# A block of the in-projection of a hybrid decoder layer: plain columns turned into seven-product form, column sets interleaved, and the token sums built from unsplit rows

## The chip, the cores and the metric

The kernel runs on one core of one Trainium2 chip. The metric is device time in microseconds (us) of one execution, the median of several; lower is better. The engines are named as in the profile: PE (matrix products), PEld (loading of PE's stationary operand), DVE (elementwise vector work), ACT (scalar functions and copies), POOL (here it issues DMAs that add into what lies at their destination), SP (issues ordinary DMAs).

## The reference, cut to what matters

One layer of a decoder on 512 tokens of width 2048. The in-projection feeds two mixers; the change touches the part of it that makes `v`.

```
shift, scale, gate = silu(c) @ W_ada + b_ada          # c: one row of 2048
h = RMSNorm(x) * (1 + scale) + shift                  # 512 x 2048
[q_lat | kv_lat | k_rope | z_mla | u | v | z_sgu | g_mla | g_sgu] = h @ W_in
    # widths 768, 512, 64, 2048, 2048, 2048, 2048, 2048, 2048
A = causal latent attention(q_lat, kv_lat, k_rope) * silu(z_mla)
B = u * (tril(W_s) @ rmsnorm(v) + b_s) * silu(z_sgu)  # chunks of 128 tokens
x = x + gate * ((sigmoid(g_mla) * A + sigmoid(g_sgu) * B) @ W_out)
out = RMSNorm(x)
```

## The kernel before, in words

**Precision.** A product of float32 matrices is made of three PE products: each operand is a high part (`hi`, rounded) and a low part (`lo` = operand minus `hi`), and `mm3` (L150 to L153) adds hi*hi, hi*lo and lo*hi into one bank of PSUM (the accumulators of PE). In the blocks below the same three stand at L638.

**The stream of weights.** Class `Stream` (L70 to L130) holds a list of granules, each up to 128 x 1024 values of a weight. A granule's raw values come by DMA into one of a few raw tiles; then it is *split*: ACT copies it into the high part (the cast, L121) and DVE subtracts that from the raw values (the low part, L122). `get(i)` splits granule i+1 while PE works on granule i, and lets DMAs run `look` granules ahead. There are two pairs of part tiles, `w0` and `w1`, so that a granule's split can't begin before PE is done with the one two places back. With `fine` the split is made in two halves; `after` keeps a granule's DMA back until another is split; `fetch` and `make` run extra DMAs or extra DVE work.

**Stages.** (1) The first weight group, `g1`. (2) The second, `g2`: 16 granules of 640 columns, one for each 128 of the 2048 rows of K. (3) The `v` stage, with which the change deals. (4) The pair stage: the other products of the in-projection, head by head, as a long row of slots of equal length. (5) Attention, the out projection, the last norm.

**Rows and fixes.** `h` is held as 16 tiles `hh[j]`, `hl[j]` (128 of K x 512 tokens). The shift of a tile is a dot product of silu(c) with a row block of W_ada on DVE (`ada_dot`, called by `dot_to`: 128 x 2048, L142). It is not there when the first products run, so `fix_to` (L464 to L491) builds the rows two tiles at a time: DVE makes `t` = x times gain and norm (two at L482 through the helper at L142), ACT adds the shift into the high parts (two at L489), DVE makes the low parts (two at L491, shown as L142). `FIXED` and `DOTS` are tables that say up to where fixes and dots have got at each granule: fixes stand in g2 at granules 4, 9, 12 and 14 and in the `v` stage at steps 0, 2, 4 and 5.

**The v stage.** 2048 columns of `v` and 64 of k_rope, 2112 in all. 1024 columns are one block made with seven products in the place of eight (2 x 2 x 2: token halves, K halves, column halves): products p1 to p7 take sums of weight quarters and sums of row quarters, each with 4 granules of two K tiles, 512 columns wide, 256 tokens. The other columns are plain: 8 granules of 384 columns, 8 more of 384, and 8 of 320, each with two K tiles and four token groups. Sums of weights are made by POOL's accumulating DMAs (p6, p2, p4) or on DVE (p3, 128 x 1024). Sums of rows (`make_sums`) are built on DVE from `hh` + `hl`: two adds of 512 and four of 256 for each of eight tiles, and then split. The stage's order is the list `plan`: 16 plain steps of 384, p1, half of the 320 ones, p6, the other half, p2, two steps for the first gate's product of head 14 (`z`), p7 and p3 in turns, p5, p4. The last four steps stand in a loop of their own at the head of the pair stage (L1357). Beside the stage, `lat_scale` (DVE, 128 x 512, 13 times) scales the latent rows and stores them, and each finished quarter of `v` is combined on DVE, squared and summed on ACT, and stored.

Of the kernel before, what the change touches and what calls it, by code (L numbers as in the profile page):

```python
# [38 lines left out]
VW = (384, 384, 320)  # L39
# [21 lines left out]
class Stream:  # L61
# [40 lines left out]
    def split_to(self, i):  # L102
        i = min(i, len(self.src) - 1)
        while self.n_split <= i:
# [6 lines left out]
            if make is not None:  # L111
                make(raw)
# [19 lines left out]
def trunk_layer(ctx, tc, xT, xn, c, vecs, pos, wada, w1, w2, wv, wv3, wv4, wh, wh15, wq, wqr, wk, wvv, wo, wsT, bsp, gfin, out,  # L132
# [111 lines left out]
    g2 = [ws.add(w2[k], 640) for k in range(KC)]  # L244
    chain = [None] * 4

    def chain_load(i):
        chain[i] = nt(c1[0].p, [P, GW], F32, f"raw{4 + i}")
        DMA.dma_start(chain[i], wv[0, i])
        return chain[i]  # L250

    def adding(src, i):
        nc.gpsimd.dma_start(chain[i], src, accum_op=ALU.add)
        return chain[i]

    b22 = [None] * 4

    def hold(i, t):
        b22[i] = t
        return t  # L260

    def kept_raw(raw):
        ws.held += 1

    def add_kept(i, raw):
        tt(raw, raw, b22[i], ALU.add)
        ws.held -= 1

    gv, last_of, steps = [], {}, []
    plan = [(kind, i) for kind, n0, n1 in ((0, 0, 8), (1, 0, 8), ("p1", 0, 4), (2, 0, 4), ("p6", 0, 4), (2, 4, 8), ("p2", 0, 4))  # L270
            for i in range(n0, n1)]
    plan += [("z", 0), ("z", 1)] + [(kind, i) for i in range(4) for kind in ("p7", "p3")]
    plan += [(kind, i) for kind in ("p5", "p4") for i in range(4)]
    for kind, i in plan:
        if kind == "z":
            g = ws.add(wh[H - 2, 0, i], GW)
        elif kind in (0, 1, 2):
            g = ws.add((wv3[0], wv3[1], wv4)[kind][i], 2 * VW[kind])
        elif kind == "p1":
            g = ws.add(None, GW, fetch=lambda t, i=i: chain_load(i), fine=True)  # L280
        elif kind in ("p6", "p2", "p4"):
            src = {"p6": wv[1, i], "p2": wv[1, 4 + i], "p4": wv[0, 4 + i]}[kind]
            g = ws.add(None, GW, fetch=lambda t, i=i, src=src: adding(src, i), after=last_of[i], fine=True)
        elif kind == "p7":
            g = ws.add(wv[1, 4 + i], GW, fetch=lambda t, i=i: hold(i, t), make=kept_raw, fine=True)
        elif kind == "p3":
            g = ws.add(wv[1, i], GW, make=lambda raw, i=i: add_kept(i, raw), fine=True)
        else:
            g = ws.add(wv[0, 4 + i], GW, fine=True)
        if kind in ("p1", "p6", "p2"):  # L290
            last_of[i] = g
        gv.append(g)
        steps.append((kind, i))
    gq, gr, gk, gvv = {}, {}, {}, {}
    c1 = [None]
# [40 lines left out]
    xp = Scope("xT")  # L336
    psp = Scope("psA", space=PSUM)
# [62 lines left out]
    def square_of(j):  # L400
        if j == 0:
            ACT.activation(ssx, xt[j], AF.Square)
            return None
        sq = nt(xp.p, [P, S], F32, "sq", bufs=2)
        ACT.activation(sq, xt[j], AF.Square)
        return sq
# [63 lines left out]
    def fix_to(n, between=None):  # L470
# [12 lines left out]
        for j in js:  # L483
            t = nt(xp.p, [P, S], F32, "t", bufs=2)
# [37 lines left out]
    S3_AT, S4_AT = ("cosT", "lat8", "lat9", "lat0"), ("sinT", "lat1", "lat7", "lat2")  # L522
    halves_, s3f, s4f = {}, {}, {}

    def half_of(tags, j):

        if j % 2 == 0:
            halves_[tags, j // 2] = nt(latp.p, [P, S], F32, tags[j // 2])
        return halves_[tags, j // 2][:, (left, right)[j % 2]]

    def make_sums(j):
        a, b = (nt(tb.p, [P, S], F32, f"t{i}") for i in range(2))
        tt(a, hh[j].bitcast(F32), hl[j].bitcast(F32), ALU.add)
        tt(b, hh[j + 8].bitcast(F32), hl[j + 8].bitcast(F32), ALU.add)
        s3f[j], s4f[j] = half_of(S3_AT, j), half_of(S4_AT, j)
        tt(s3f[j], a[:, left], a[:, right], ALU.subtract)
        tt(b[:, right], a[:, right], b[:, right], ALU.subtract)
        tt(a[:, left], b[:, right], a[:, left], ALU.subtract)
        tt(s4f[j], a[:, left], b[:, left], ALU.add)

        def split():
            for name, src in (("s1", b[:, right]), ("s2", a[:, left])):
                hilo(sums[name + "h"][:, j], sums[name + "l"][:, j], src)

        return split

    def split_s4(j):
        hilo(sums["s4"][:, j, 0], sums["s4"][:, j, 1], s4f[j])

    def split_s3(j):  # L550
        hilo(hh[j][:, right], hl[j][:, right], s3f[j])
# [15 lines left out]
    for t_, i in zip((8, 9, 10, 11, 12, 13, 16, 17, 24, 25, 26, 28, 30), (8, 1, 9, 7, 12, 10, 0, 2, 3, 4, 11, 5, 6)):  # L567
        early.setdefault(t_, []).append(lambda i=i: lat_scale(i))

    def sums_begin(j, t_):  # L570
        early.setdefault(t_ + 1, []).insert(0, make_sums(j))

    for j, t_ in enumerate((9, 11, 12, 14, 15, 20, 21, 22)):
        early.setdefault(t_, []).append(lambda j=j, t_=t_: sums_begin(j, t_))
# [1285 lines left out]
```

## Time and profile before

| what | value |
|---|---|
| time, median of 3 runs (lowest, highest) | 1549.36 us (1549.21, 1549.51) |
| the profiled execution's own time | 1549.69 us |
| its span on the core | 1548.0 us |
| what lies around the span | 1.69 us |
| granted clock of PE, mean | 0.998 |
| g1 | 0 to 98.5 us |
| g2 | 98.97 to 153.81 us |
| v stage | 153.81 to 336.72 us |
| pair stage | 336.72 to about 1080 us |
| attention and out projection | about 1080 us to the end |

A row of the timeline gives start, duration, engine, line, operation, output<-inputs, shapes, and how many instructions it stands for; what stands in brackets is idle time ahead of it on its engine and what ended it. A row of groups gives count, then after the bar busy time in us, the mean of one in ns, and the idle time ahead. A row of windows gives the stretch, its length, and for PE, PEld, DVE, ACT and POOL the busy time (and instructions), then the granted clock, the busy share of the 16 DMA engines and GB/s.

### The profile page before, as it was taken

To read this page: it belongs to the slowest core of one execution; us is meant where nothing else is said; L and a number is where in the kernel's file an instruction comes from. 1 tells how busy PE (TensorE), PEld (TensorE's weight loads), DVE (VectorE), ACT (ScalarE), POOL (GpSimd) and SP (SyncE) were. 2 spreads that over 40 slices of the span, in tenths; PEclk is the share of its full clock that TensorE was granted. 3 is DMA by queue.
4 is the path that set the end of the run, shared out by engine and by line. 5 is a ranking of instruction groups with operands and counts; after the bars stand their busy time and mean duration, and the time that the engine had idled before them with its cause. 6 is when DMAs were issued, how large, how long until landed. Compare 5 with 4: busy or idle time off the path is not lost.

```text
span 1548.0 us, 27203 instructions
## 1 busy us (share of the span) xinstructions
PE 1535.9 (99%) x10680; PEld 1431.5 (92%) x10680; DVE 1176.7 (76%) x1808; ACT 764.4 (49%) x1331; POOL 104.6 (7%) x128
## 2 busy tenths in 40 slices
PE   9999999999999999999999999999999999999997
PEld 7888999889999999999999999999888888888887
DVE  8989787568787888877778777777788888854543
ACT  4443454555645454454555546555655555632322
POOL 0000001001111111111111111121000000000000
PEclk9999999999999999999999999999999999999999
DMA  9978387758999999997888888888544344245423
GB/s 376 386 272 311 121 241 220 178 177 210 279 267 280 251 250 252 267 264 206 222 234 251 221 246 242 223 204 219 164 143 131 129 125 145 81 163 189 136 82 109
DMA packets 129394, 327.57 MB, mean 212 GB/s; under 512 B 14809, under 2 KB 36337, under 8 KB 124529
## 3 DMA queue, kind: packets, MB, share of 16 engines
q1 hardware_dynamic: 112114, 270.52, 50.9%
q0 software_dynamic: 17008, 55.06, 19.8%
q8 instruction: 84, 1.38, 0.4%
q14 instruction: 44, 0.36, 0.1%
q10 hardware_dynamic: 144, 0.26, 0.1%
HBM read 301.85 MB, written 23.94 MB: 210 GB/s over the span
## 4 chain that ended last, share of the span: by engine, by line
PE 95%; DMA 2%; DVE 1%; ACT 0%; SPq 0%; issue 0%; DVEq 0%; ACTq 0%
PE ps L1410 15%; PE ps L1411 15%; PE ps L1412 15%; PE ps L152 14%; PE ps L153 14%; PE ps L151 14%; PE ps L638 4%; PE ps L1589 1%; PE ps L970 1%; DMA wraw<-in_w 1%; PE ps L1553 1%; PE ps L1552 1%; DMA half<-in_pos 1%; DMA v_d<-lat 0%; DMA wada<-in_wada 0%
## 5 line engine op out<-in xcount | busy, mean ns | idle before, releaser
L1410 PE MATMUL ps<-h,w2h 128*128 128x256 f32 x408 | 113.8, 279 | 0.0
L1410 PE MATMUL ps<-h,w0h 128*128 128x256 f32 x408 | 113.1, 277 | 0.7 <-DVE lat L139 0.7
L1412 PE MATMUL ps<-h,w2l 128*128 128x256 f32 x408 | 112.7, 276 | 0.0
L1412 PE MATMUL ps<-h,w0l 128*128 128x256 f32 x408 | 112.7, 276 | 0.0
L1411 PE MATMUL ps<-h,w2h 128*128 128x256 f32 x408 | 112.7, 276 | 0.0
L1411 PE MATMUL ps<-h,w0h 128*128 128x256 f32 x408 | 112.7, 276 | 0.0
L1410 PE MATMUL ps<-h,w1h 128*128 128x256 f32 x400 | 110.9, 277 | 0.0
L1412 PE MATMUL ps<-h,w1l 128*128 128x256 f32 x400 | 110.5, 276 | 0.0
L1411 PE MATMUL ps<-h,w1h 128*128 128x256 f32 x400 | 110.5, 276 | 0.0
L122 DVE TENSOR_TENSOR w0l<-wraw,w0h 128x1024 fp32r<-128x1024 f32 (+3 forms) x70 | 71.5, 1024 | 47.3 <-ACT w0h L121 47.0
L122 DVE TENSOR_TENSOR w1l<-wraw,w1h 128x1024 fp32r<-128x1024 f32 (+3 forms) x71 | 65.5, 928 | 51.0 <-ACT w1h L121 49.8
L121 ACT CAST w1h<-wraw 128x1024 fp32r<-128x1024 f32 (+3 forms) x71 | 57.4, 814 | 93.1 <-PE ps L153 33.1
L121 ACT CAST w0h<-wraw 128x1024 fp32r<-128x1024 f32 (+3 forms) x70 | 62.7, 899 | 81.7 <-PE ps L153 36.5
L139 DVE TENSOR_TENSOR w0l<-raw,w0h 128x1024 fp32r<-128x1024 f32 x56 | 68.5, 1224 | 32.6 <-ACT w0h L796 31.8
L151 PE MATMUL ps<-h,w1h 128*128 128x512 f32 x218 | 86.6, 397 | 0.0
L153 PE MATMUL ps<-h,w1l 128*128 128x512 f32 x218 | 85.0, 390 | 0.0
L152 PE MATMUL ps<-h,w1h 128*128 128x512 f32 x218 | 85.0, 390 | 0.0
L139 DVE TENSOR_TENSOR w1l<-wraw,w1h 128x1024 fp32r<-128x1024 f32 x44 | 53.9, 1225 | 36.4 <-ACT w1h L796 36.4
L139 DVE TENSOR_TENSOR w2l<-wraw,w2h 128x1024 fp32r<-128x1024 f32 x46 | 56.3, 1224 | 29.9 <-ACT w2h L796 29.8
L151 PE MATMUL ps<-h,w0h 128*128 128x512 f32 x198 | 78.0, 394 | 0.0
L152 PE MATMUL ps<-h,w0h 128*128 128x512 f32 x198 | 77.2, 390 | 0.5 <-DVE h L142 0.5
L774 POOL DMA_DIRECT2D wraw<-in_wh x55 | 49.3, 958 | 417.6 <-DVE w1l L139 153.3
(418 smaller groups left out, 5462.3 us busy)
## 6 DMA issues: line engine op xcount, KB each, us to landing
raw<-in_wh SPq DMA_DIRECT2D x104, 512.0 KB, 6.9
wada<-in_wada SPq DMA_DIRECT2D x31, 1024.0 KB, 6.8
wraw<-in_wh POOLq DMA_DIRECT2D x55, 512.0 KB, 8.3
wraw<-in_wh SPq DMA_DIRECT2D x45, 512.0 KB, 6.1
raw<-in_wh POOLq DMA_DIRECT2D x36, 512.0 KB, 7.5
wraw<-in_wo SPq DMA_DIRECT2D x32, 512.0 KB, 3.7
half<-in_w SPq DMA_DIRECT2D x35, 256.0 KB, 5.6
wraw<-in_w SPq DMA_DIRECT2D x16, 512.0 KB, 8.4
```

The costliest lines, as they stand in the source:

```text
L121: self.nc.scalar.copy(hi[:, sl], raw[:, sl])
L122: self.nc.vector.tensor_tensor(out=lo[:, sl], in0=raw[:, sl], in1=hi[:, sl].bitcast(F32), op=ALU.subtract)
L139: DVE.tensor_tensor(out=out, in0=in0, in1=in1, op=op)
L151: PE.matmul(ps, ah, bh, start=start, stop=False)
L152: PE.matmul(ps, ah, bl, start=False, stop=False)
L153: PE.matmul(ps, al, bh, start=False, stop=stop)
L638: PE.matmul(ps, x_[:, tk], w_[:, sl], start=st and m == 0, stop=c == 7 and m == 2, skip_group_check=True)
L774: q_.dma_start(t, wh[h, n, q // 10 - 1], **eng)
L970: PE.matmul(ps[:, n], v[:, n], wr[:, q], start=True, stop=True)
L1410: PE.matmul(ps[:, :256], wH[:, cols[c]], xh, start=c == 0 and first, stop=False, skip_group_check=True)
L1411: PE.matmul(ps[:, :256], wH[:, cols[c]], xl, start=False, stop=False, skip_group_check=True)
L1412: PE.matmul(ps[:, :256], wL[:, cols[c]], xh, start=False, stop=c == 7, skip_group_check=True)
```

## The change

All columns of `v` but 256 (320 with k_rope) are now made with seven products: set `a` (columns 0 to 1023, halves of 512) and set `b` (columns 1024 to 1791, halves of 384; these were the 16 plain granules of 384). Both sets use the same sums of rows. The plain 320 columns go first, the `z` product of head 14 next, and then the two sets in turns.

- **Order of the steps** (4 granules each but for v and z): v 0 to 7, z 8 and 9, a1 10 to 13, b1 14 to 17, a5 18 to 21, b5 22 to 25, a6 26 to 29, a7 30 to 33, a2 34 to 37, a3 38 to 41, a4 42 to 45, b6 46 to 49, b7 50 to 53, b2 54 to 57, b3 58 to 61, b4 62 to 65 (the last four in the loop at the pair stage's head).
- **Sums of weights.** a6: an ordinary load into a chain tile and an accumulating DMA onto it. a2, a4, b2, b4: an accumulating DMA onto the chain tile. a3, b3: an ordinary load and an accumulating one. b6: two ordinary loads, added on DVE (128 x 768). So 28 accumulating DMAs stand in the stage (16 of 512 KB, 12 of 384 KB) where 12 stood.
- **Sums of rows.** `fix_to` gets one more instruction for each tile: ACT writes t + shift back into `xt[j]`, so that the unsplit row stays. `make_sums` is then four DVE instructions of 256 for each of eight tiles, each using what the one ahead of it made, and `split_sums` four casts on ACT and four lows on DVE, one step later.
- **Side work.** `lat_scale` is moved to steps 8, 30 to 37, 42, 44, 46 and 48; the combining of quarters (`corner`) is put on numbered steps. `FIXED` and `DOTS` are unchanged.

```diff
-VW = (384, 384, 320)
+VW = {"a": 512, "b": 384, "v": 320}
+V0 = {"a": 0, "b": 1024, "v": 1792}
...
+    def onto(t, src):
+        nc.gpsimd.dma_start(t, src, accum_op=ALU.add)
+    def chain_load(i, c, n):
+        chain[i] = t = nt(c1[0].p, [P, GW], F32, f"raw{4 + i}")
+        DMA.dma_start(t[:, :n], wpair[c][0, i])
+        if c == "a":
+            onto(t[:, :n], wpair[c][1, i])
+        return t
+    def add_raw(i, raw, n):
+        tt(chain[i][:, :n], chain[i][:, :n], raw[:, :n], ALU.add)
         return chain[i]
...
+    steps = [("v", "", i) for i in range(8)]
+    for kind in ("z", "a1", "b1", "a5", "b5", "a6", "a7", "a2", "a3", "a4", "b6", "b7", "b2", "b3", "b4"):
+        steps += [(kind[0], kind[1:], i) for i in range(2 if kind == "z" else 4)]
...
         for j, t in zip(js, ts_):
             stt(hl[j], t, shift[:, j:j + 1], hh[j].bitcast(F32), ALU.add, ALU.subtract)
+            ACT.activation(xt[j], t, AF.Identity, bias=shift[:, j:j + 1])
...
     def make_sums(j):
-        a, b = (nt(tb.p, [P, S], F32, f"t{i}") for i in range(2))
-        tt(a, hh[j].bitcast(F32), hl[j].bitcast(F32), ALU.add)
-        tt(b, hh[j + 8].bitcast(F32), hl[j + 8].bitcast(F32), ALU.add)
-        s3f[j], s4f[j] = half_of(S3_AT, j), half_of(S4_AT, j)
...
+        u, v = xt[j], xt[j + 8]
+        a, b = temps[j] = [nt(xq.p, [P, S], F32, "t", bufs=2) for _ in range(2)]
+        tt(a[:, left], u[:, right], v[:, right], ALU.subtract)
+        tt(a[:, right], a[:, left], u[:, left], ALU.subtract)
+        tt(b[:, left], a[:, right], v[:, left], ALU.add)
+        tt(b[:, right], u[:, left], u[:, right], ALU.subtract)
+    def split_sums(j):
+        a, b = temps.pop(j)
+        s1, s2 = sums_of[j] = [nt(xp.p, [P, 2, 256], F32R, f"x{c}") for c in (j, j + 8)]
+        hilo(s1[:, 0], s1[:, 1], a[:, left])
+        hilo(s2[:, 0], s2[:, 1], a[:, right])
+        hilo(sums["s4"][:, j, 0], sums["s4"][:, j, 1], b[:, left])
+        hilo(hh[j][:, right], hl[j][:, right], b[:, right])
...
+    for j, t_ in enumerate((8, 9, 11, 13, 15, 18, 20, 23)):
+        at_step(t_, make_sums, j)
+        at_step(t_ + 1, split_sums, j)
+    for t_, i in zip((8, 30, 31, 32, 33, 34, 35, 36, 37, 42, 44, 46, 48), (11, 0, 2, 8, 9, 7, 1, 12, 3, 10, 4, 5, 6)):
+        at_step(t_, lat_scale, i)
+    for n in range(2):
+        for t_, f, *a in ((20, keep_v, "a", "1", n), (22, corner, "a", n, "11"), (24, keep_v, "b", "1", n), (26, corner, "b", n, "11"),
...
+                          (42, keep_v, "a", "3", n), (43, corner, "a", n, "22"), (46, corner, "a", n, "21"),
```

**Place 1: ACT at the second fix of g2.** `w0h` and `w1h` are high parts of weights, `wraw` a raw tile, `h` the high parts of the rows, `t` what DVE made for them. Before, ACT has:

```order
L121 CAST w0h_1225<-wraw_26_1159 128x640
L489 ACTIVATE h_137_1251<-t_1247,shift_88 128x512
L489 ACTIVATE h_138_1253<-t_1249,shift_88 128x512
L121 CAST w1h_1257<-wraw_27_1183 128x640
L121 CAST w0h_1281<-wraw_28_1207 128x640
```

After, on the same engine at the same place (`x` is the row tile that is kept, and the lines of the file have moved):

```order
L122 CAST w0h_1230<-wraw_26_1164 128x640
L495 ACTIVATE h_137_1256<-t_1252,shift_88 128x512
L495 ACTIVATE h_138_1258<-t_1254,shift_88 128x512
L500 ACTIVATE x_40_173<-t_1252,shift_88 128x512
L500 ACTIVATE x_41_174<-t_1254,shift_88 128x512
L122 CAST w1h_1264<-wraw_27_1188 128x640
L122 CAST w0h_1288<-wraw_28_1212 128x640
```

Two instructions have come in between the high parts of the rows and the next weight's cast.

**Place 2: DVE around b6 (steps 46 to 49).** `raw` is a chain tile, `wraw` the second load, `lat<-lat,rx` is `lat_scale`, `lat<-ps,lat` a corner; `x2` are the two halves of a split. Before, at the p7 and p3 steps, which held the DVE additions of weights there:

```order
L122 TENSOR_TENSOR w0l_2700<-w2l_2440,w0h_2699 128x512 x2
L139 TENSOR_TENSOR wraw_71_2475<-wraw_71_2475,w2l_2440 128x1024
L122 TENSOR_TENSOR w1l_2733<-wraw_71_2475,w1h_2732 128x512 x2
L139 TENSOR_TENSOR h_130_1125<-cosT_1802,h_130_1125 128x256
L139 TENSOR_TENSOR h_131_1127<-cosT_1802,h_131_1127 128x256
L122 TENSOR_TENSOR w0l_2761<-wraw_72_2510,w0h_2760 128x512 x2
```

After:

```order
L140 TENSOR_TENSOR raw_239_2672<-raw_239_2672,wraw_79_2670 128x768
L123 TENSOR_TENSOR w1l_2770<-raw_239_2672,w1h_2769 128x384 x2
L140 TENSOR_TENSOR lat_26_137<-lat_26_137,rx_93 128x512
L140 TENSOR_TENSOR lat_240_2687<-ps_182_1844,lat_240_2687 128x512
L140 TENSOR_TENSOR raw_241_2698<-raw_241_2698,wraw_80_2696 128x768
L123 TENSOR_TENSOR w0l_2796<-raw_241_2698,w0h_2795 128x384 x2
L140 TENSOR_TENSOR lat_242_2714<-ps_183_1845,lat_242_2714 128x512
L140 TENSOR_TENSOR raw_243_2725<-raw_243_2725,wraw_81_2723 128x768
L123 TENSOR_TENSOR w1l_2824<-raw_243_2725,w1h_2823 128x384 x2
```

The additions stood at every second granule and now stand at four in a row, with `lat_scale` and the corners between them.

**Place 3: DVE at steps 23 and 24.** `t<-x,...` are the sums of rows of the eighth tile, `sinT<-ps,sinT` is a corner. The row pieces before stood elsewhere (each sum between the splits of two plain granules). After:

```order
L123 TENSOR_TENSOR w0l_2230<-w2l_2081,w0h_2229 128x384 x2
L140 TENSOR_TENSOR t_2249<-x_45_178,x_53_186 128x256
L140 TENSOR_TENSOR t_2249<-t_2249,x_45_178 128x256
L140 TENSOR_TENSOR t_2250<-t_2249,x_53_186 128x256
L140 TENSOR_TENSOR t_2250<-x_45_178 128x256
L140 TENSOR_TENSOR sinT_2203<-ps_205_2084,sinT_2203 128x512
L123 TENSOR_TENSOR w1l_2259<-wraw_57_2109,w1h_2258 128x384 x2
```

Four sums and a corner stand between the splits of two granules of set b.

More of the change, by code (lines that the diff above doesn't have):

```diff
@@ L611, in quarter, with of_sums @@
     def quarter(c0, toks):
         return lambda c: (hh[c0 + c][:, toks], hl[c0 + c][:, toks])
[L614 to L628 removed]
+    def of_sums(e):
+        return lambda c: (sums_of[c][e][:, 0], sums_of[c][e][:, 1])
@@ L629, in block @@
+    rights = {1: quarter(0, left), 2: of_sums(1), 3: quarter(0, right), 4: quarter(8, right),
+              5: quarter(8, left), 6: of_sums(0), 7: lambda c: (sums["s4"][:, c, 0], sums["s4"][:, c, 1])}
+    z14 = [None]
+    def keep_z14():
+        z14[0] = keep(latp.p, "lat11", psv["z"][0])
+    def block(c, p, i, wH, wL):
+        w = VW[c]
+        key = c + ("y" if p in "124" else p)
+        opens = p in "13567"
+        if i == 0 and opens:
+            open_banks(key, w)
         for k in range(2):
-            c = 2 * i + k
@@ L660, in trunk_layer, with run_step @@
+    def run_step(t_, wH, wL):
+        c, p, i = steps[t_]
+        if c == "v":
+            w = VW[c]
             if i == 0:
-                psv[kind] = [bank()[:, :w] for _ in range(4)]
+                open_banks(c, w)
             for k in range(2):
```

290 lines of the change are left out of this document (126 added, 164 removed).

## The prediction

> **What bounds the kernel now.** I read the page first, then the windows by stage, then the timelines of PE, DVE and ACT around one fix, then the groups of the v stage and the DMA queues.
>
> ```profile
> span 1548.0 us, 27203 instructions
> PE 1535.9 (99%) x10680; PEld 1431.5 (92%) x10680; DVE 1176.7 (76%) x1808; ACT 764.4 (49%) x1331; POOL 104.6 (7%) x128
> 98.50:153.80 55.30, 55.30 (x243) 45.42 (x242) 51.23 (x63) 19.49 (x28) 0.00 (x0) 1.00 0.85 317
> 153.80:336.70 182.90, 182.73 (x961) 166.55 (x960) 128.33 (x215) 90.31 (x183) 10.33 (x12) 1.00 0.63 180
> ```
>
> PE is busy 99% of the span, so fewer products can show in the time. But g2 (98.50 to 153.80) has DVE at 51.23 of 55.30 us, so DVE there is nearly as full as PE. The v stage is wide open by its mean: DVE 128.33 of 182.90, DMA 0.63. A mean says nothing of a place, so each place that the change touches is worked out below. The profiled execution took 1549.69 us, 0.33 above the median of 1549.36; the sum is made against the former and 0.33 is taken off at the end.
>
> **PE's work.** The pitch of a granule is read from the starts of like first products.
>
> ```profile
> 130.01 0.39 PE L151 MATMUL ps<-h,w1h 128*128 128x512 f32 x1
> 133.41 0.39 PE L151 MATMUL ps<-h,w0h 128*128 128x512 f32 x1
> 153.81 0.33 PE L151 MATMUL ps<-w0h,h 128*128 128x384 f32 x1
> 158.00 0.33 PE L151 MATMUL ps<-w1h,h 128*128 128x384 f32 x1
> 162.16 0.33 PE L151 MATMUL ps<-w0h,h 128*128 128x384 f32 x1
> 231.32 0.30 PE L151 MATMUL ps<-w0h,h 128*128 128x320 f32 x1
> 234.84 0.31 PE L151 MATMUL ps<-w1h,h 128*128 128x320 f32 x1
> 220.56 10.92 PE ps L638 x48
> ```
>
> A g2 granule takes 3.40 us, a plain one of 384 takes 4.16 (24 products, 173 ns each), one of 320 takes 3.52, a block granule of 512 takes 10.92 / 4 = 2.73 (12 products; 2.72 is used, as in 10.88 for four). A block granule of 384 has 12 products of 173 ns: 2.08. The z granule has 24 products of 512, 24 x 0.227 = 5.44. Before: 16 x 4.16 + 8 x 3.52 + 2 x 5.44 + 28 x 2.72 = 181.8. After: 8 x 3.52 + 2 x 5.44 + 28 x 2.72 + 28 x 2.08 = 173.4. **Gain 8.3 us** (rounded once), which is 48 products. The stage lasted 182.9 (153.81 to 336.72), so 1.1 us of stalls lay in it; they belong to the old order, and since every stall of the new one is counted below, they go: **gain 1.1**.
>
> **The front: g2 and the plain steps.** Here is DVE around g2's second fix, with ACT beside it.
>
> ```profile
> 128.09 2.29 DVE L142 SCALAR_TENSOR_TENSOR wada<-wada,cact 128x2048 f32<-128x2048 f32 x1
> 130.30 0.08 DVE L142 DVE_READ_ACCUMULATOR wada<-wada,cact 128x1 f32 x1
> 130.75 0.82 DVE L122 TENSOR_TENSOR w0l<-wraw,w0h 128x640 fp32r<-128x640 f32 x1 [0.36 <-ACT w0h L121]
> 131.49 0.15 DVE L139 TENSOR_TENSOR shift<-dots,vec 128x2 f32<-128x2 f32 x1
> 131.56 1.41 DVE L142 SCALAR_TENSOR_TENSOR t<-x,gxA,rx 128x512 f32<-128x512 f32 x2
> 133.10 1.42 DVE L142 SCALAR_TENSOR_TENSOR h<-t,shift,h 128x512 fp32r<-128x512 f32 x2
> 134.44 0.82 DVE L122 TENSOR_TENSOR w1l<-wraw,w1h 128x640 fp32r<-128x640 f32 x1
> 135.17 2.28 DVE L142 SCALAR_TENSOR_TENSOR wada<-wada,cact 128x2048 f32<-128x2048 f32 x1
> 132.34 1.39 ACT L489 ACTIVATE h<-t,shift 128x512 fp32r<-128x512 f32 x2 [1.62 <-DVE t L142]
> 133.64 0.71 ACT L121 CAST w1h<-wraw 128x640 fp32r<-128x640 f32 x1
> ```
>
> DVE goes without a gap: t, low parts, the next weight's low part, a dot. ACT's cast for that weight starts at 133.64, as soon as the two h's are through, and DVE's low part follows it at 134.44: 2.88 us after t began. The change puts two more instructions of the h's kind between h's and cast. The two h's took 132.34 to 133.64, so the copies take 1.3, and DVE's low part starts 4.15 after t's start: 1.27 later. Behind it DVE has the dots, and PE the next granule. Seven of the eight fixes pay this; at v step 4 a dot stands between t and the low parts on DVE and covers the copies.
>
> The DVE chain from fix to fix: 4.15 for a fix up to the next low part, 0.74 for a low part (134.44 to 135.17), 2.37 for a dot with its read. The first fix's delay of 1.27 less an idle 0.46 starts the second one at 132.35 in the place of 131.56; three granules and two dots on, the third at 143.4; then one dot and two low parts between each two (8.0): 151.4, 159.4 (v step 0), 167.4 (step 2), 175.4 (step 4). Step 4's fix has its dot inside (1.4 + 2.4 + 1.4, and a low part, 5.9), so step 5's starts at 181.3, step 7's low part at 185.4, and it ends at 186.2. PE without stalls would begin step 7 at 153.81 + 7 x 3.52 = 178.45. **Cost 7.7**. Half of it comes from the copies, the rest because the plain steps are now 3.52 and not 4.16 long while dots and fixes are as many.
>
> ```profile
> L142 DVE SCALAR_TENSOR_TENSOR wada<-wada,cact 128x2048 f32<-128x2048 f32 x4 | 9.1, 2285 | 0.0
> L142 DVE SCALAR_TENSOR_TENSOR h<-t,shift,h 128x512 fp32r<-128x512 f32 x8 | 5.7, 749 | 0.4
> L142 DVE SCALAR_TENSOR_TENSOR t<-x,gxA,rx 128x512 f32<-128x512 f32 x8 | 5.6, 747 | 0.0
> ```
>
> Its bounds: without the copies the v stage has 9.1 + 0.3 of dots, 11.9 of fixes with their shifts and five low parts (3.7), 25 us, against 6 x 3.52 = 21.1 of PE; less a slack of 0.9 to 1.9 (the lead of a split over its granule) that is a cost of 2 at the least. With all eight copies uncovered and none of DVE's idle 4.1 us of g2 left over it is 3.9 + 10.2 - 4.1 - 0.9 = 9.1 at the most. I take the chain.
>
> **Steps 22 to 26.** From the groups of the v stage:
>
> ```profile
> L122 DVE TENSOR_TENSOR w1l<-raw,w1h 128x512 fp32r<-128x512 f32 x16 | 10.3, 687 | 4.9 <-ACT w1h L121 4.9
> L139 DVE TENSOR_TENSOR t<-t,t 128x256 f32<-128x256 f32 x16 | 6.8, 422 | 0.3
> L139 DVE TENSOR_TENSOR lat<-lat,rx 128x512 f32<-128x512 f32 x13 | 8.9, 684 | 0.0
> L122 DVE TENSOR_TENSOR w1l<-wraw,w1h 128x768 fp32r<-128x768 f32 x7 | 6.7, 957 | 5.1 <-ACT w1h L121 5.1
> L121 ACT CAST w1h<-raw 128x512 fp32r<-128x512 f32 x16 | 9.1, 618 | 8.5 <-PE ps L153 3.2 <-issue 2.4 <-PE ps L638 2.1
> L605 ACT ACTIVATE ps<-lat 128x512 f32<-128x512 f32 x4 | 2.4, 598 | 4.4 <-DVE lat L139 4.4
> ```
>
> At step 23 DVE has four sums (4 x 0.42 = 1.6) and then a corner (0.65); ACT's square of that corner (0.6) stands ahead of the cast for step 25 (384 wide, about 0.5), whose low part (about 0.5) ends the chain: 3.9, with handovers 4.2. The steps are 2.08 long, so PE waits some 2.3 before step 25, and 0.7 more before 26, whose cast stands behind the casts of the sums. **Cost 3.0**; bounds 0 (if the lead of the splits took it all) and 3.6.
>
> **b6, steps 46 to 49.** Each granule needs, one after the other, a DVE addition of 768 (0.96 by the low part of 768), a cast (0.5) and two low parts of 384 (two at about 0.5 by the 512's 0.69 less overlap): 2.7 with handovers, in steps of 2.08. Between them stand `lat_scale` and corners, 0.61 to 0.68 each, three of them inside the run. 4 x 2.7 + 3 x 0.63 = 12.7 against 4 x 2.08 = 8.3 leaves 4.4, less a lead of some 1.6: **cost 2.75**; bounds 0 and 4.4.
>
> **The end of the stage.** The last block step is 2.08 and not 2.72 long, and slot 1 of the pair stage splits 128 x 1024 beside it.
>
> ```profile
> 336.70:372.00 35.30, 34.50 (x297) 33.96 (x296) 25.60 (x41) 20.77 (x36) 4.80 (x5) 1.00 0.83 242
> ```
>
> PE lost 0.8 of 35.3 us there before. The shorter step makes slot 1's split 0.6 late, and corners at 60 to 63 add 0.2: **cost 0.8**, between -0.9 (all present loss gone) and 2.
>
> **DMA.** The window of the v stage first, then 420 to 440 us, with its window row.
>
> ```profile
> q1 hardware_dynamic: 10936, 26.48, 43.4%
> q0 software_dynamic: 1728, 6.29, 19.3%
> ...
> q1 hardware_dynamic: 1969, 4.85, 63.2%
> q0 software_dynamic: 442, 1.59, 40.0%
> 420.00:440.00 20.00, 20.00 (x178) 20.00 (x178) 17.23 (x23) 8.34 (x11) 1.70 (x2) 1.00 1.04 324
> ```
>
> Accumulating: 6.29 MB in 19.3% of 182.9 us, 178 GB/s; plain 334. In the full stretch of 20 us it is 1.59 MB in 8.0 us, 199, and 384. From step 17 on the change moves 13.1 MB accumulating (16 x 0.524 + 12 x 0.393) and about 21.4 plain (12 x 0.524 + 16 x 0.393 of weights, 6.7 of stores, 2.1 for the first slots). At the full stretch's rates that is 66 + 56 = 122 us; at the stage's, 74 + 64 = 138. PE has 2.08 + 24 x 2.72 + 24 x 2.08 = 117 us there, 123 with the waits above. Since the faster rates were seen when the engines were full, as they would be here, I take them: it just fits, **cost 1**, bounds 0 and 15.
>
> ```profile
> raw<-in_wv POOLq DMA_DIRECT2D x12, 512.0 KB, 6.6
> wraw<-in_wv SPq DMA_DIRECT2D x7, 512.0 KB, 3.5
> ```
>
> An accumulating 512 KB landed 6.6 us after its issue, a plain one 3.5 (window 153.8 to 372). The Trainium skill ("DMA: Bandwidth & Descriptors", the section on the anatomy of a gpsimd DMA) gives 2.0 us and bytes over 436 GB/s, 3.2 us for 512 KB; by that all 34.5 MB would be 79 us of transfer and no bound at all. The rows differ by twice for the accumulating ones, and the rows decide.
>
> **Sum.** -8.3 - 1.1 + 7.7 + 3.0 + 2.75 + 0.8 + 1 = +5.85. 1549.69 + 5.85 - 0.33 = 1555.2 us.
>
> **Rivals.** Beside the forecast, slower by 0.38%:
>
> 1. *Only the front binds.* The split of a granule leads it, and DVE has 54 us of idle time in the stage to build a lead in the a steps. If the leads take steps 22 to 26, b6 and the end: -8.3 - 1.1 + 7.7 = -1.7, 1547.7 us, no change. For it: the a steps leave DVE 1 us and more each. Against it: there are two part buffers, so a lead is at most one granule, and b6's chain is longer than a step four times running.
> 2. *PE's work alone decides.* If the copies and dots hide (ACT is busy only 19.49 of 55.30 us in g2) and the rest too: -9.4, 1540.0 us, faster. Against it: ACT's queue, in order, has the copies ahead of the cast whatever its share.
> 3. *DMA becomes the bound.* At the stage's mean rates the accumulating queue makes the tail of 138 us longer than 123: +15 in the place of +1, 1569 us. It decides as soon as the engines' need passes the time of PE, which 122 against 123 nearly does. Against it: the full stretch at 420 us, in which PE didn't wait.
> 4. *The clock.* Granted clock is 1.00 in every window quoted. The Trainium skill ("TensorE: Matmul & The Clock Gate", on HAM oscillation) says that a gap of over about 3.4 us lets the clock fall to half. The longest wait forecast here is 2.4 us (before step 5's granule, 178.9 to 181.3), so I leave the clock alone. If a gap of the front did lower it for some us, 3 to 6 more: 1558 to 1561.
>
> That the change doesn't do what it says isn't likely: the 48 products are gone from PE's order.
>
> **How the numbers follow.** A measurement of this kernel can tell 0.2%, 3.1 us, from no change, so "same" is 1546.3 to 1552.5. Forecast 0.60 (of it 0.08 below 1552.5, where two of the bounded costs vanish), rival 1 0.18 (0.02 of it under 1546.3), rival 2 0.10, rival 3 0.10, rival 4 0.02. Faster 0.10 + 0.02 = 0.12; same 0.16 + 0.08 = 0.24; slower 0.52 + 0.10 + 0.02 = 0.64. The forecast's own range is 1550 to 1561. The range leaves out rival 2 and most of rival 3: 1546.5 to 1563.
>
> **What would show it.** In the trace after: products of 384 in blocks at 173 ns; the second fix's cast 1.3 us later behind two new ACT rows; step 7's first product near 186 us, with PE's idle time ended by DVE's low parts; waits of about 2.3 us before step 25 and of 0.6 to 1 before steps 47 to 49; the DMA share from step 17 above 0.9 with few PE waits on DMA. I'm wrong if step 7 starts within 2 us of 178.5 (copies hidden), if no wait stands at b6, or if PE's idle time in the tail ends with landings of accumulating DMAs.

## The result, and the profile after

| | before | after |
|---|---|---|
| median (lowest to highest), us | 1549.34 (1549.21 to 1549.51) | 1557.65 (1556.84 to 1559.16) |
| profiled execution, us | 1549.69 | 1558.15 |
| span, us | 1548.0 | 1556.4 |
| v stage | 153.81 to 336.72: 182.9 us | 153.8 to 344.0: 190.2 us |
| from there to the end | 1211.3 us | 1212.4 us |

The ratio is 1.0055, 95% interval 1.0037 to 1.0072: slower by 0.55%, 8.3 us, where 5.85 were forecast. The page of the kernel after, and its windows: g2, the whole v stage, its last 100 us, and 4.4 us in the middle (columns as before: PE, PEld, DVE, ACT, POOL, then granted clock, DMA share, GB/s).

```profile
span 1556.4 us, 27283 instructions
PE 1536.3 (99%) x10632; PEld 1425.6 (92%) x10632; DVE 1185.0 (76%) x1846; ACT 784.4 (50%) x1387; POOL 116.7 (7%) x144
98.50:153.80 55.30, 55.30 (x242) 45.07 (x241) 48.84 (x61) 23.60 (x36) 0.00 (x0) 1.00 0.83 311
153.80:344.00 190.20, 181.90 (x914) 159.75 (x913) 136.78 (x250) 106.56 (x235) 24.08 (x28) 0.99 0.84 237
237.00:241.40 4.40, 3.92 (x13) 3.66 (x14) 3.66 (x8) 3.71 (x10) 0.00 (x0) 0.65 1.05 278
240.00:340.00 100.00, 97.14 (x463) 83.81 (x463) 63.66 (x109) 50.82 (x110) 20.54 (x24) 0.99 1.06 282
```

PE's busy time in the page (1536.3, before 1535.9) hides the whole change: there are 48 products fewer, and in the stage's window PE is idle for 8.3 us only, though the pitches add up to 173.4 of the 190.2 us. The starts of the granules tell more. They show the pitches of the forecast, 3.52, 5.44, 2.72 and 2.08 us, wherever nothing waits, and lost time at five places. Start-to-start time of the granules over their pitch, summed by place, gives this account (us; a landing is the end of a DMA transfer):

| term | forecast | measured |
|---|---|---|
| PE's work, 48 products fewer | -8.3 | -8.3 |
| stalls of the old order | -1.1 | -1.1 |
| front, up to the first z granule | +7.7 | +6.0 |
| steps 22 to 26 | +3.0 | +2.0, and +1.9 by a low clock |
| b6, with the a4 granule ahead of it | +2.75 | +4.2 |
| waits on landings (DMA) | +1 | +2.0 |
| end of the stage and all behind it | +0.8 | +1.4 |
| others | | +0.4 |
| sum | +5.85 | +8.5 (spans: +8.4) |

**The front.** DVE at g2's second fix after the change, then ACT there:

```profile
131.93 1.41 DVE L143 SCALAR_TENSOR_TENSOR t<-x,gxA,rx 128x512 f32<-128x512 f32 x2
133.47 1.42 DVE L143 SCALAR_TENSOR_TENSOR h<-t,shift,h 128x512 fp32r<-128x512 f32 x2
135.98 0.82 DVE L123 TENSOR_TENSOR w1l<-wraw,w1h 128x640 fp32r<-128x640 f32 x1 [1.09 <-ACT w1h L122]
136.72 2.29 DVE L143 SCALAR_TENSOR_TENSOR wada<-wada,cact 128x2048 f32<-128x2048 f32 x1
132.71 1.39 ACT L495 ACTIVATE h<-t,shift 128x512 fp32r<-128x512 f32 x2 [1.90 <-DVE t L143]
134.01 1.32 ACT L500 ACTIVATE x<-t,shift 128x512 f32<-128x512 f32 x2
135.24 0.71 ACT L122 CAST w1h<-wraw 128x640 fp32r<-128x640 f32 x1
```

The two copies (x at 134.01) stand where the order had them, and DVE waits 1.09 us for the cast behind them. The low part starts 4.05 us after t, where it was 2.88: the same 1.09 stands at seven of the eight fixes. PE at the plain steps 6 and 7 and at the first z granule:

```profile
179.64 0.41 PE L153 MATMUL ps<-w0l,h 128*128 128x320 f32 x1 [1.26 <-DVE w0l L123]
183.63 0.41 PE L152 MATMUL ps<-w1h,h 128*128 128x320 f32 x1 [0.35 <-ACT w1h L122]
184.49 0.42 PE L153 MATMUL ps<-w1l,h 128*128 128x320 f32 x1 [0.45 <-DVE w1l L123]
187.96 0.39 PE L152 MATMUL ps<-h,w0h 128*128 128x512 f32 x1
```

PE waits for low parts, and the z granule starts at 187.96 in the place of 153.81 + 8 x 3.52 = 181.97: 6.0 late.

**Step 25.** DVE, ACT and PE around it:

```profile
233.85 0.42 DVE L140 TENSOR_TENSOR t<-x,x 128x256 f32<-128x256 f32 x1
234.30 0.89 DVE L140 TENSOR_TENSOR t<-t,x 128x256 f32<-128x256 f32 x2
235.10 0.42 DVE L140 TENSOR_TENSOR t<-x 128x256 f32<-128x256 f32 x1
235.44 0.68 DVE L140 TENSOR_TENSOR sinT<-ps,sinT 128x512 f32<-128x512 f32 x1
236.16 0.60 ACT L589 ACTIVATE ps<-sinT 128x512 f32<-128x512 f32 x1 [2.87 <-DVE sinT L140]
236.78 0.91 ACT L122 CAST w1h<-wraw 128x384 fp32r<-128x384 f32 x2
237.33 0.44 PE L649 MATMUL ps<-w1h,h 128*128 128x384 f32 x1 [1.58 <-ACT w1h L122]
```

The chain is the one forecast: four sums, the corner, its square, the cast. PE lost 1.8 us. What follows wasn't in the sum: the granule at 237.33 takes 4.00 us and not 2.08, because the granted clock falls to 0.65 (the window from 237.00 above).

**b6.** DVE (a corner, an addition, two low parts), ACT's cast, PE:

```profile
301.43 0.68 DVE L140 TENSOR_TENSOR lat<-ps,lat 128x512 f32<-128x512 f32 x1
302.03 0.95 DVE L140 TENSOR_TENSOR raw<-raw,wraw 128x768 f32<-128x768 f32 x1
303.64 1.03 DVE L123 TENSOR_TENSOR w0l<-raw,w0h 128x384 fp32r<-128x384 f32 x2 [0.66 <-ACT w0h L122]
303.09 0.93 ACT L122 CAST w0h<-raw 128x384 fp32r<-128x384 f32 x2 [0.22 <-DVE raw L140]
303.66 0.44 PE L649 MATMUL ps<-w0h,x 128*128 128x384 f32 x1 [0.96 <-ACT w0h L122]
```

Addition, cast, low parts follow one another in 2.55 us (302.03 to 304.58) for a step of 2.08, with the corner ahead.

**DMA.** The queues in the v stage, and two of the five casts that waited for a landing (the others, of a6 at 246.12 and 249.34 and of b2 at 315.55, waited 0.65, 0.15 and 1.61):

```profile
q1 hardware_dynamic: 12547, 31.74, 48.3%
q0 software_dynamic: 4032, 13.11, 35.4%
...
242.41 1.14 ACT L122 CAST w1h<-raw 128x512 fp32r<-128x512 f32 x2 [1.70 <-DMA raw<-in_wv]
312.63 0.93 ACT L122 CAST w0h<-wraw 128x384 fp32r<-128x384 f32 x2 [1.72 <-DMA wraw<-in_wv]
```

13.11 MB accumulating, as counted. From 240 to 340 us the engines are full (1.06) at 282 GB/s, where before they were at 0.63 at the like place (240 to 336.7). The 345 plain and 195 accumulating GB/s of the stage (31.74 MB in 91.9 us, 13.11 in 67.3) lie between the two pairs of rates in the prediction; the accumulating one is near the full stretch's, the plain one near the stage's before.

The landings themselves say more than the share. The eight accumulating DMAs of a3 and a4 (512 KB each) were issued between 260.9 and 272.2 us and landed between 269.6 and 292.05, one every 3.2 us, while PE takes a granule of 512 in 2.72. So in this stretch a landing follows the transfers ahead of it and not its own issue, and a cast that comes earlier has to wait for it.

### The profile page after: what moved, and what is told of

The parts are those of the page before. It is cut to its first block, busy times and chain, and to the rows that moved or that the text cites. A ratio compares the mean times of both kernels' runs of the same rounds, so it can differ in the third digit from the quotient of the medians.

```text
span 1556.4 us, 27283 instructions
## 1 busy us (share of the span) xinstructions
PE 1536.3 (99%) x10632; PEld 1425.6 (92%) x10632; DVE 1185.0 (76%) x1846; ACT 784.4 (50%) x1387; POOL 116.7 (7%) x144
## 4 chain that ended last, share of the span: by engine, by line
PE 90%; DMA 4%; DVE 3%; ACT 2%; issue 1%; SPq 0%; POOL 0%; DVEq 0%; ACTq 0%; POOLq 0%
PE ps L1418 15%; PE ps L1419 15%; PE ps L1420 15%; PE ps L153 12%; PE ps L154 12%; PE ps L152 12%; PE ps L649 5%; DMA raw<-in_wv 1%; PE ps L1597 1%; PE ps L983 1%; DMA wraw<-in_wv 1%; DMA wraw<-in_w 1%; DMA v_d<-lat 1%; DVE w0l L123 1%; PE ps L1561 1%
## 5 line engine op out<-in xcount | busy, mean ns | idle before, releaser
L123 DVE TENSOR_TENSOR w0l<-wraw,w0h 128x1024 fp32r<-128x1024 f32 (+4 forms) x78 | 73.4, 952 | 48.5 <-ACT w0h L122 48.1
L122 ACT CAST w0h<-wraw 128x1024 fp32r<-128x1024 f32 (+4 forms) x78 | 64.5, 839 | 75.9 <-PE ps L154 25.3
L123 DVE TENSOR_TENSOR w1l<-wraw,w1h 128x512 fp32r<-128x512 f32 (+4 forms) x76 | 66.0, 878 | 47.5 <-ACT w1h L122 46.3
L122 ACT CAST w1h<-wraw 128x512 fp32r<-128x512 f32 (+4 forms) x76 | 57.9, 773 | 75.3 <-PE ps L154 28.6
L152 PE MATMUL ps<-h,w0h 128*128 128x512 f32 x198 | 78.0, 394 | 0.0
L154 PE MATMUL ps<-h,w0l 128*128 128x512 f32 x198 | 77.6, 392 | 0.0
```

Of the source, the lines that this page charges most:

```text
L122: self.nc.scalar.copy(hi[:, sl], raw[:, sl])
L123: self.nc.vector.tensor_tensor(out=lo[:, sl], in0=raw[:, sl], in1=hi[:, sl].bitcast(F32), op=ALU.subtract)
L152: PE.matmul(ps, ah, bh, start=start, stop=False)
L154: PE.matmul(ps, al, bh, start=False, stop=stop)
```

## The experiments

Each is compared with runs of the kernel before on the same chip; the change itself is 1557.65 us, ratio 1.0055.

**Copies behind the cast.** `fix_to` notes the copies and they are issued after the next `get`:

```diff
-            ACT.activation(xt[j], t, AF.Identity, bias=shift[:, j:j + 1])
+            copies.append((j, t))
...
         wH, wL = get(gv[t_])
+        copy_rows()
```

> The 16 row copies on ACT are put behind the next granule's cast; nothing is left out. Front theory (copies ahead of the cast make each low part 1.1 us late): the low part starts some 2.9 us after t as before, and the front's cost falls from 6.0 us to about 2, what is left being the shorter plain steps; 1553.6 us. Rival (the copies are hidden, DVE is simply too full for steps of 3.52): the first z granule still starts near 188 us, 1557 us.

1552.72 us, ratio 1.0020 (1.0012 to 1.0029): 4.9 us less than the change. DVE and ACT at the second fix:

```profile
131.69 1.41 DVE L143 SCALAR_TENSOR_TENSOR t<-x,gxA,rx 128x512 f32<-128x512 f32 x2
134.57 0.82 DVE L123 TENSOR_TENSOR w1l<-wraw,w1h 128x640 fp32r<-128x640 f32 x1
133.77 0.71 ACT L122 CAST w1h<-wraw 128x640 fp32r<-128x640 f32 x1
134.38 1.34 ACT L479 ACTIVATE x<-t,shift 128x512 f32<-128x512 f32 x2
```

The low part is back at 2.88 after t, and the same 16 copies do the same work 0.6 us later. The first z granule starts at 182.82, so the front's cost falls from 6.0 to 0.85. So the copies' place made nearly all of it, more than the 4 expected; the shorter plain steps alone fit. Most of the 5.1 us won in the front reaches the pair stage, which starts 4.9 us earlier. Between, the clock didn't fall at step 25 (1.4 us less), but a6 lost 2.3 us and a4 2.0, where the change had 1.2 and 0.45; casts that waited for a landing stand in both places.

**z between.** The first z granule goes ahead of plain step 4 (and the first copy of a `v` bank, with its square, one step later).

```diff
+    steps.insert(4, steps.pop(8))
```

> The first z granule (5.44 us of PE for 1.2 us of DVE) goes between the plain steps 3 and 4; copies as in the change. Front theory: only the waits ahead of the fourth plain step stay (about 2.2 us), those behind it (some 3.8) are covered by the z granule's room; 1554 us. Rival (each fix stalls PE on its own, however much room there is): all waits stay, 1557.5 us.

1556.89 us, ratio 1.0046 (1.0033 to 1.0059). Neither came out. The waits ahead of the z granule and at it were 3.5 us and not 2.2, since z's own low part (128 x 1024) is longer, and 1.2 stayed behind it: 4.7 in the place of 5.9. In this trace the pair stage starts at 342.01, 2.0 us earlier than in the change; the last granule of a4 waited 1.2 us in the place of 0.45, and b7 and b2 0.3 in the place of 1.0. By the median the whole is 0.8 us shorter, with intervals that overlap. A wide step lends room only to what comes behind it; it doesn't shorten the queue that makes a fix late.

**The copies alone, in the kernel before.**

```diff
             stt(hl[j], t, shift[:, j:j + 1], hh[j].bitcast(F32), ALU.add, ALU.subtract)
+            ACT.activation(xt[j], t, AF.Identity, bias=shift[:, j:j + 1])
```

> The kernel before with the 16 row copies alone, at the place where the change puts them; what they write is read by nothing. Theory that copies and short steps bind only together: two plain granules of 384 give PE 8.3 us for DVE's 7.8, so most is covered; 0.5 to 1.5 us over before, about 1550.3 us. Rival (a copy pair costs its 1.1 us wherever it stands): 6 us or more over before, 1555 us.

1552.19 us, ratio 1.0017 (1.0008 to 1.0026): 2.7 us over the kernel before, between the two. The waits of 0.8 (end of g2), 0.95 (first plain granule), 0.3 and 0.95 (at 180 and 184 us) make 3.0. So the longer plain steps of 4.16 us cover about half of what the copies cost in the change, and not as much as expected.

**The last row sum later.**

```diff
-    for j, t_ in enumerate((8, 9, 11, 13, 15, 18, 20, 23)):
+    for j, t_ in enumerate((8, 9, 11, 13, 15, 18, 20, 25)):
```

> The eighth row sum is made at step 25 and split at 26 in the place of 23 and 24; nothing is left out. Theory: the wait of 1.8 us before step 25 and the slow clock behind it (1.9 us at a granted clock of 0.65) both go, some 1 us comes back at step 26: about 1555 us. Rival (DVE is full from step 8 to 25 as a whole, so a wait only moves): 1557 us, with a wait of 1.5 us or more elsewhere in steps 25 to 28.

1557.40 us, ratio 1.0053 (1.0041 to 1.0066): no gain, as the rival had it, but not for the rival's reason. The wait before step 25 went (0.2), and the clock stayed at 1.00. In their place a6's first two casts waited for their data:

```profile
238.03 1.14 ACT L122 CAST w0h<-raw 128x512 fp32r<-128x512 f32 x2 [1.88 <-DMA raw<-in_wv]
241.84 1.14 ACT L122 CAST w1h<-raw 128x512 fp32r<-128x512 f32 x2 [2.30 <-DMA raw<-in_wv]
```

The second cast started at 242.41 in the change and at 241.84 here: the landing sets it, whatever DVE does before. Steps 24 to 29 lose 4.9 us in both.

**b6's side work moved out.**

```diff
-    for t_, i in zip((8, 30, 31, 32, 33, 34, 35, 36, 37, 42, 44, 46, 48), (11, 0, 2, 8, 9, 7, 1, 12, 3, 10, 4, 5, 6)):
+    for t_, i in zip((8, 30, 31, 32, 33, 34, 35, 36, 37, 42, 44, 52, 54), (11, 0, 2, 8, 9, 7, 1, 12, 3, 10, 4, 5, 6)):
...
-                          (42, keep_v, "a", "3", n), (43, corner, "a", n, "22"), (46, corner, "a", n, "21"),
+                          (42, keep_v, "a", "3", n), (43, corner, "a", n, "22"), (50, corner, "a", n, "21"),
```

> The corners of steps 46 and 47 go to 50 and 51, lat_scale of steps 46 and 48 to 52 and 54; nothing is left out. DVE theory: b6's waits fall from 4.2 to about 2 us (2.6 us of chain in steps of 2.08), 1555.5 us. Rival (the DMA engines are full from 240 to 340 us, so PE would wait for data instead): what b6 gives is taken by waits on landings at b7 to b3, 1557.5 us.

1559.52 us, ratio 1.0066 (1.0054 to 1.0078): nothing gained. The waits of b6's four granules fell from 3.7 to 2.0 us, just as DVE's chain said. But those at b7 and b2 grew from 1.0 to 1.5, and no cast there waits for a landing any more: each stands behind the square of a corner that was moved there, and the square waits for DVE. From b6's first product to the pair stage's first the trace has 45.3 us, where the change has 46.65, so 1.3 us are won where the edit acts. They are lost at places that lie ahead of the moved work: at a6 (2.8, were 1.2), where the clock didn't fall at step 25 (1.4 us less) and the casts waited for landings instead, and at a4 (2.2, was 0.45). So the pair stage starts at 344.27, 0.3 us later than in the change. A cast of a6 and one of a4, then the first square at b7 and the cast behind it:

```profile
249.18 1.14 ACT L122 CAST w1h<-raw 128x512 fp32r<-128x512 f32 x2 [0.66 <-DMA raw<-in_wv]
...
290.59 1.14 ACT L122 CAST w0h<-raw 128x512 fp32r<-128x512 f32 x2 [1.84 <-DMA raw<-in_wv]
...
311.64 0.60 ACT L589 ACTIVATE ps<-lat 128x512 f32<-128x512 f32 x1 [1.28 <-DVE lat L140]
312.63 0.93 ACT L122 CAST w0h<-wraw 128x384 fp32r<-128x384 f32 x2
```

So the rival's mechanism didn't come out: behind b6 nothing was given back to landings. Why a4 waited longer in this execution isn't shown.

**a6's transfers early.**

```diff
-                    g = ws.add(None, n, fetch=lambda t, f=f: f(t)[0], fine=True)
+                    g = ws.add(None, n, fetch=lambda t, i=i: chain[i], fine=True)
...
+    for i in range(4):
+        at_step(12 + i, chain_load, i, "a", 2 * VW["a"])
```

> The loads and accumulating DMAs of a6 are issued at steps 12 to 15 and not when the stream reaches them (about step 20); nothing is left out. DMA theory: the four waits on landings (a6, 0.2 + 0.45 + 0.5, and b7/b2, 0.5 + 0.55) go, 2 us less, 1555.6 us, with the DMA share under 1 near the end of the stage. Rival (the later waits are latency of single transfers): the a6 waits alone go, 1 us, 1556.6 us.

1559.58 us, ratio 1.0064 (1.0052 to 1.0076): both wrong. The landings at a6 and b7 are in time, but the early transfers went ahead of those for a5 and b5, whose casts now waited 2.5 and 2.7 us; the waits from 223 to 244 us are 7.5, where the change had 4.9 from 233 to 251, each with a low clock in it.

**Both.** The edits of the two runs above together.

> Both edits: b6's side work moved out and a6's transfers early. If DMA is what holds b6 (rival), the pair gains 4 us where the first alone gains nothing: 1553.5 us. If DVE holds b6, the gains add: 2 and 2, 1553.5 us as well, but then the first alone shows 2.

1558.72 us, ratio 1.0060 (1.0047 to 1.0073): the waits at a5 and b5 stay (7.2 from 226 to 244 us), b6's are 2.0. At b7 and b2 the waits are 1.5, where the run with a6's transfers early alone has none; no cast there waits for a landing in either. So of the 1.8 us that b6 gave, 1.5 went with the moved corners to b7. The pair doesn't gain what DVE's theory adds up, nor the 4 us of the other.

**a6's accumulating DMAs left out**, on top of the copies behind the cast:

```diff
         if c == "a":
-            onto(t[:, :n], wpair[c][1, i])
+            pass
```

> The kernel with the copies behind the cast, and a6's four accumulating DMAs (512 KB each) left out, so the set's a6 and what follows is computed from one quarter of the weights only. DMA theory: some 10 us of engine time less while the engines are full; the waits at a6 (0.5 + 1.1 + 0.6) and the extra ones at a4 (0.7 + 1.3 in the place of 0.45) go, DMA share under 1 between 240 and 300 us: about 1549 us, 3.7 under the kernel with the copies behind the cast (1552.7). Rival (those waits are made by ACT and DVE queues): within 0.7 us of 1552.7.

1552.41 us, ratio 1.0019 (1.0011 to 1.0028), against 1552.72: by time, the rival. By the trace, DMA: no cast of the stage waits for a landing, and the pair stage starts at 336.41 in the place of 339.13. That is 2.7 us earlier (0.5 of it because the stage starts earlier), though this execution lost 1 us to a low clock at step 25. Of the 2.7 us, 1.2 are lost behind the stage (1214.6 us from there to the end, 1213.4 in the other profile). The share from 240 to 336 us was still 1.00, so the expectation of less was wrong, and a share of 1.00 doesn't by itself make PE wait. With executions from 1550.45 to 1554.05, the time shows neither theory.

**All five edits.**

> All five edits: copies behind the cast, z between, last row sum late, b6's side work out, a6's transfers early. If each wait has its own cause: 6.0 + 2.9 + 2.1 + 2 less, 1544.6 us, under the kernel before. Rival (the DMA engines need some 122 us from step 17 on, so what the front and steps 22 to 26 give is lost in the tail): 1549 us or more, with long waits on landings between b6 and b3.

1551.45 us, ratio 1.0012 (1.0004 to 1.0021): 6.2 us less than the change, and still over the kernel before. The front has no wait left, so z between does help once the copies are out of the way. But the waits from 212 to 250 us are 5.5 (the longest behind late data at a5 and b5, as with a6's transfers early alone), b6's 2.0, b7's and b2's 1.5 (behind the moved corners, as above). The rival had the time of this one, though not the place: it put the waits between b6 and b3.

**lat_scale on POOL**, at steps 0 to 8, on top of the copies behind the cast; **and the best of each** (that, with the last sum late and b6's corners moved).

```diff
-        tt(lat[i], lat[i], rx, ALU.mult)
+        nc.gpsimd.tensor_tensor(out=lat[i], in0=lat[i], in1=rx, op=ALU.mult)
```

> The kernel with the copies behind the cast, and the 13 lat_scale multiplications on POOL at steps 0 to 8, with their stores, in the place of DVE at steps 8 and 30 to 48; nothing is left out. DMA theory: 3.1 MB of stores move from the full stretch to 160 to 200 us (8 us of engine time), and b6 loses two of its side instructions: 1552.7 - 2 - 1 = 1549.7 us. Rival (POOL's work slows DVE's, which is full there): low parts and fixes between 154 and 190 us get longer, waits of some us come back in the front, 1553 us or more.

> Copies behind the cast, last row sum late, b6's corners at 50 and 51, lat_scale on POOL early; nothing is left out. If front, steps 22 to 26, b6 and DMA each give what they are thought to: 1552.7 - 2 (no waits of 1.8 before step 25) - 2 (b6) - 2 (DMA) = 1546.7 us, 0.2% under the kernel before. Rival (DMA stays full whatever is moved): 1550 us or more.

1564.76 us, ratio 1.0098 (1.0084 to 1.0111), and 1564.10, ratio 1.0096 (1.0081 to 1.0112): 12 us lost by the move. The multiplications stand at steps 0 to 8 in the program, but POOL has nothing ahead of them, and eight ran in one go in g2, as soon as their data was there. POOL, DVE and PE there, in the first of the two runs:

```profile
111.86 14.75 POOL L566 TENSOR_TENSOR lat<-lat,rx 128x512 f32<-128x512 f32 x8 [102.35 <-DVE rx L525]
115.60 1.24 DVE L140 TENSOR_TENSOR shift<-dots,vec 128x2 f32<-128x2 f32 x1
116.77 3.55 DVE L143 SCALAR_TENSOR_TENSOR t<-x,gxA,rx 128x512 f32<-128x512 f32 x2
121.73 0.50 PE L152 MATMUL ps<-h,w0h 128*128 128x512 f32 x1 [2.45 <-ACT w0h L122]
125.53 0.80 PE L154 MATMUL ps<-h,w0l 128*128 128x512 f32 x1 [3.06 <-DVE w0l L123]
```

The two t's take 3.55 us and not 1.41, and the waits of PE are followed by a low clock. The `v` stage starts at 161.39, where the run with the copies alone moved has 153.95: 7.4 of the 12 us are lost here, ahead of the stretch that the rival had in mind. POOL, then DVE, in the plain steps:

```profile
167.43 1.50 POOL L566 TENSOR_TENSOR lat<-lat,rx 128x512 f32<-128x512 f32 x1 [3.27 <-ACT lat L529]
167.69 3.39 DVE L143 SCALAR_TENSOR_TENSOR wada<-wada,cact 128x2048 f32<-128x2048 f32 x1
171.01 1.90 DVE L123 TENSOR_TENSOR w1l<-wraw,w1h 128x640 fp32r<-128x640 f32 x1
```

A dot takes 3.39 us and not 2.29, a low part 1.90 and not 0.82, and in g2 the tiny `shift` 1.24 and not 0.15: each DVE instruction that starts beside one of POOL's is some 1.1 us longer, the short ones as the long ones. The plain steps lose 5.7 us more (a low clock in it). That is the rival's mechanism, dearer than it was thought. The Trainium skill ("SBUF — State Buffer", on who interferes with whom) says that a DVE instruction with two inputs in SBUF contends with a GpSimd one that reads SBUF; the rows agree.

The DMA theory holds a part too. From the first z granule to the pair stage the first run takes 153.5 us, where the run with the copies alone moved takes 156.3: the waits at a6 fell from 2.3 to 0.8, a4 has none, and b6 lost 0.8 less. In the second run the wait before step 25 and the low clock went, but a6's waits came back (4.6 us up to step 29, with two casts behind landings), as with the last sum late alone; this stretch takes 154.05.

**All edits, with the transfers earlier still** (a6 at steps 8 to 11, eight of the scalings on DVE at steps 6 and 7).

> The kernel with all five edits (1551.45 us), but a6's transfers at steps 8 to 11 in the place of 12 to 15, and eight of the lat_scale multiplications on DVE at steps 6 and 7 (the last plain ones) in the place of 30 to 37, with their stores; nothing is left out. DMA theory: 15.6 us of a6's engine time and 5.4 of stores move into 175 to 205 us, where the DMA share is 0.3 to 0.7; the waits on landings at a5 and b5 (0.5 + 1.0 + 0.5 + 0.7) and at b7 and b2 (0.9 + 0.5) go: 1547.5 us, just under the kernel before. Rival (DMA stays full from 200 us on and only the place of the waits moves): 1550.5 us or more.

1555.12 us, ratio 1.0032 (1.0020 to 1.0044). The waits from 220 to 260 us did shrink (0.2 + 0.5 + 0.3 + 0.6 + 0.2, where all five edits had 5.5), but one of a new kind came:

```profile
204.80 0.59 ACT L572 COPY lat<-ps 128x512 f32<-128x512 f32 x1 [7.79 <-DMA lat_d<-lat]
```

ACT's copy of the z product goes into the tile of latent row 11, whose store stood behind the early traffic; with ACT held for 7.8 us, every cast behind it waited, and steps 12 and 13 lost 8.0 us. This place is the experiment's own fault. What the earlier transfers are worth isn't shown by it, since the DMA engines had those 8 us to get ahead; with another tile it may come under the kernel before, but that wasn't run.

## Why the prediction was right

It forecast slower by 0.38% with the chance 0.64, and 0.55% was measured, inside the range. The places where time is lost were right, and that is not luck; that the sum came within 2.5 us is in part. The front and steps 22 to 26 were together 2.7 us too dear, while b6, the DMA and the end were 3.0 too cheap and the clock's 1.9 stood at nothing. Point by point:

- **PE's work**: right to 0.1 us.
- **Front** (7.7 forecast, 6.0 measured): the mechanism and the place were right, shown by the copies alone moved. The size was off for two reasons. The chain took a dot with its read at 2.37 us, but the next instruction starts 2.21 behind the dot, so fixes stand 7.8 and not 8.0 us apart; and PE starts a granule when its high part is there (183.63), before the low part is (its first low product starts at 184.49). "Half of it comes from the copies, the rest because the plain steps are now 3.52" was wrong: with the copies moved 0.85 is left, so shorter steps alone cost next to nothing; the copies alone, beside the longer steps, cost 3.0; and the rest of the 6.0 needs both.
- **Steps 22 to 26** (3.0): the chain was right; it measured 1.8 and 0.2. The low clock behind it, 1.9, was the fourth rival's mechanism at a place where the sum counted a wait of only 2.3, and it had the chance 0.02.
- **b6** (2.75): the mechanism was right, the lead of 1.6 us wasn't there. A corner and a `lat_scale` ahead of it (294.5 to 295.7) had used it up, and PE lost 4.2 of the 4.4 that the bound allowed.
- **End** (0.8): 1.4.
- **DMA** (1): 2.0 by the waits, one half at a6, the other at b7 and b2. The prediction named PE waits that end with landings of accumulating DMAs as a sign of being wrong, and at a6 that sign came, if small: the casts at 242.41 and 246.12. What the sum had wrong is that it treats this term and the one of steps 22 to 26 as free of each other. Where a6's casts start is set by landings, so waits ahead of them cost nothing more. Two pairs of runs show it: steps 24 to 29 lose 4.9 us in the change and 4.9 with the last sum late; with `lat_scale` on POOL they lose 4.5, and 4.8 when the late sum is added. The low clock is covered in the same way: where it didn't come, with the copies moved and with b6's side work out, these steps lose 4.6 and 5.1.

For b6 the same isn't shown. Its side work moved out gave 1.8 us there, and 0.5 to 1.5 of it was lost at b7 to the same corners and not to landings.

That a6 and a4 wait for the transfers rests on the traces: casts that start at a landing, landings one every 3.2 us, and no such cast when four accumulating DMAs are left out. Whether the 16 engines or the queue of accumulating DMAs alone sets those 3.2 us wasn't separated. By the time alone it isn't settled, since the median of the run that leaves them out hardly moved. Why the time from the pair stage on varies by 1 to 3 us between profiles (1211.3 to 1214.6) stays open.

## What to carry to other kernels

An instruction added to an engine that is half idle isn't free if that engine's queue has a cast behind it that a full engine waits for: put it behind that cast. Before waits are added up as costs, or taken out as gains, look at the landings behind them: a wait ahead of a cast that its landing holds back anyway is worth nothing, and the two are one budget. Work that is moved out of a tight place takes its cost along, so look at the place where it goes. An engine that had nothing ahead in its queue ran its work as soon as the data was there, in g2 (POOL at 111.86 us) and not in the stage in which the program has it. Here 48 products fewer brought nothing: the sums and transfers that replace them took the 8.3 us back on ACT, DVE and DMA, and even with all five edits the kernel stays 2.0 us over the one before.

## What the runs showed of the hardware

- The granted clock fell after a wait in which PE lost 1.8 us (1.58 of them idle). The Trainium skill ("TensorE: Matmul & The Clock Gate", on HAM oscillation) puts the bound at gaps of over about 3.4 us; the runs here show it at half of that. From 238.30 to 241.70 us it was 0.50. Two windows around the wait at step 25, of the kernel after, and then of the one with the copies behind the cast (where the wait lies in the first window):

```profile
226.00:234.00 8.00, 8.00 (x43) 7.39 (x42) 6.57 (x17) 5.18 (x13) 3.54 (x4) 1.00 1.00 361
234.00:242.00 8.00, 6.27 (x25) 5.58 (x25) 5.72 (x13) 4.55 (x12) 0.56 (x1) 0.79 1.05 274
```

```profile
226.00:234.00 8.00, 6.25 (x35) 5.64 (x34) 5.55 (x13) 4.52 (x13) 2.27 (x3) 1.00 1.05 292
234.00:242.00 8.00, 7.54 (x33) 5.67 (x32) 4.77 (x9) 4.48 (x10) 1.70 (x2) 1.00 1.07 272
```

  The same wait of 1.8 us is followed by a low clock in one and not in the other; of six profiled executions with it, four showed it, and so did two in which step 24 lost 2.3 us (1.6 idle). In the kernel after, the waits of 1.5 us (179.64) and 1.6 us (first additions of b6) weren't followed by it.
- A POOL multiplication of 128 x 512 beside DVE adds some 1.1 us to a DVE instruction that starts beside it, to one of 0.15 us as to one of 2.29 (rows above).
- Accumulating DMAs of 512 KB that are under way together, with the engines at 1.06, landed one every 3.2 us (a3 and a4 of the kernel after); the median from issue to landing in that stage was 12.6 us, where it was 6.6 before.
